# Entry of an experts' loop: the order of its first loads, splits and gate transfers

## The chip, the cores and the metric

One core of a Trainium2 chip runs the whole layer as one program. The metric is the device time of an execution in microseconds (us). "Before" and "change" are two programs that compute the same layer.

## What is computed

The reference is one layer of a streaming encoder: two token mixers (a gated DeltaNet and an HGRN2), merged by gates, then a product-key expert mixer, then a norm. The change lies where the mixer over experts begins. Cut to that part:

```
def _peer(x, w_pq, sub_keys, expert_u, expert_v):   # 512 tokens, D = 1024
    q = (xf @ w_pq).reshape(n_tok, P_HEADS, 2, P_DHALF)
    s = einsum('thpd,phkd->thpk', q, sub_keys)      # 8 heads, 2 x 128 keys
    ... top 16 of 256 candidate pairs of each head: idx, gate
    h = gelu(einsum('td,tkd->tk', xt, expert_u[idx]))
    y = einsum('tk,tkd->td', gate * h, expert_v[idx])
```

The kernel does this densely for the first 368 tokens: it computes h for all 16384 experts, multiplies by a gate that is zero nearly everywhere, and multiplies by all of expert_v. The other 144 tokens gather their own rows of expert_u and expert_v.

## The kernel before, in words

The 16384 experts are 128 blocks of 128. For a block b, TensorE makes h (128 experts by 368 tokens) from 8 x 3 matmuls, because each float32 operand is split in a high and a low part that TensorE takes as fp32r, and three of the four products are kept. ScalarE puts GELU(h) into one of 30 slots (tiles hext and ogA). Later block m multiplies its slot by the gates of its 128 experts (hg, line 1728), splits the product into wh and wl and the block of expert_v into vh and vl, and TensorE adds 18 matmuls into six accumulators y (y_part, y_mm). The products are taken in the order wh with vh, wh with vl, wl with vh, so the second matmul of a block needs vl, and the third wl.

Blocks 0 to 29 of h are made ahead of the loop, as filler for TensorE while the top-16 lists are formed and turned into dense gates. spread (line 1572 on) writes these gates, 12 slices of 32 tokens, to gD in DRAM: each slice goes through half of the tile stage, and of the last slice only the first 16 experts of each block row (256 KB) are written at once; the rest of it (1792 KB, called the gates' rest here) stays in stage for later.

The loop (line 1785) runs from i = -3 to 127, with n = i + 3. Each step loads block n of expert_v (v_load, line 1702) and the weights of h block n + 30 (w_load, line 482), issues gathers for the other tokens on GpSimd (line 1660), prepares block i + 1 (prep, line 1717) and gives TensorE the 18 y matmuls of block i and then the 24 matmuls of h block i + 30. Gates come back from gD four blocks at a time (g_load, line 1690): the first gate read, for blocks 0 to 3, on SyncE's queue, and the later ones on ScalarE's. Of these the second, for blocks 4 to 7, is issued at i = -1; its target lies in stage where the gates' rest still stands, and it reads rows of the rest too, so it waits for the write of the rest. This write (line 1807) follows at n = 1, and a one-element copy on GpSimd (line 1805, the probe), which reads the first gates and writes into stage, holds it until the first gate read has landed.

Splitting weights (w_split, line 485) is a copy on ScalarE for the high part (whi) and, for the low part (wlo), either a subtraction on VectorE or GpSimd, or, with eng None, a second ScalarE copy of -whi and an accumulating DMA from GpSimd's queue that adds the raw weights. The last 42 weights before the loop take the last way (w_cut).

prep for block 0 makes vh and wh on VectorE, for all others on ScalarE. Its order is hg, high parts, the split of h block m + 30, one gathered row if there is one (consume), wl, vl.

Every engine works its instructions in the order in which they are written in the source; in_order at the end of build fixes it. v 0, v 1, ... are blocks of expert_v, and h block 30 + m is made right behind the y part of block m.

Of the kernel before, what the change touches and what calls it, by code (L numbers as in the profile page):

```python
# [22 lines left out]
P = 128  # L23
# [20 lines left out]
NPRE = 30  # L44
# [29 lines left out]
NDMA = 4  # L74
# [5 lines left out]
GLEAD = 5  # L80
LAG = 2
GB = 4
# [197 lines left out]
def build(ctx, tc, I, O):  # L280
    nc = tc.nc
# [5 lines left out]
    def act(o, i, f, **kw):  # L287
        nc.scalar.activation(o, i, f, **kw)  # L288

    vec, gps, pe = nc.vector, nc.gpsimd, nc.tensor  # L290
# [172 lines left out]
    order = []  # L463
    for h in range(H):
        us = [(k, h) for k in HEAD]
# [6 lines left out]
    N0 = len(order)  # L472
# [5 lines left out]
    raws, wts = {}, {}  # L478

    def w_load(src):  # L480
        raw = wpool.tile([P, DC, UW], F32, tag="wraw", name="wraw")
        nc.sync.dma_start(raw, src)
        return raw

    def w_split(raw, eng=gps):
        hi = wpool.tile([P, DC, UW], F32R, tag="whi", name="whi")
        lo = wpool.tile([P, DC, UW], F32R, tag="wlo", name="wlo")
        act(hi, raw, AF.Copy)
        if eng is None:

            act(lo, hi.bitcast(F32), AF.Copy, scale=-1.0)
            gps.dma_start(out=lo, in_=raw, accum_op=OP.add)
        else:
            eng.tensor_tensor(lo, raw, hi.bitcast(F32), OP.subtract)  # L494
        return hi, lo
# [5 lines left out]

    def w_cut(n):
        if n < len(order):
            wts[n] = w_split(raws.pop(n), vec if n < 2 else gps if n < N0 + NDMA else None)

    def piece(p, w, c, m):
        whi, wlo = w
# [8 lines left out]
    with ExitStack() as ph:  # L516
        sb = ph.enter_context(tc.tile_pool(name="sb", bufs=1))

        def sbt(tag, bufs=1, shape=(P, T), dt=F32):
            return sb.tile(list(shape), dt, tag=tag, name=tag, bufs=bufs)  # L520
# [530 lines left out]
        for k in range((NF - 1) * DC):  # L1051
            n, c = 1 + k // DC, k % DC
            if n > NF - 3:

                c, n = divmod(k - (NF - 3) * DC, 2)
# [71 lines left out]
    with ExitStack() as ph:  # L1127
# [46 lines left out]
        for n in range(NPROJ, N0):  # L1174
# [10 lines left out]
            m = {"w_a": (ohi, olo), "w_b": hm, "w_out": (mhi, mlo)}.get(kind, hm)  # L1185
# [20 lines left out]
    gg2 = hk.tile([P, KP], F32, name="gg2")  # L1206
# [8 lines left out]
    def u_mm(uh, ul, p=None, part=(0, 3 * DC)):  # L1215
        p = psh.tile([P, ND], F32, tag="h", name="h") if p is None else p
        for i in range(*part):
            c, k = divmod(i, 3)
            mm(p[:, 0:NM], (uh, ul, uh)[k][:, c, :], (hhi, hhi, hlo)[k][:, c, 0:NM], i == 0, i == 3 * DC - 1)
        return p  # L1220

    def u_act(b, p):
        act(slots[b % NPRE][:, 0:NM], p[:, 0:NM], AF.Gelu)
# [10 lines left out]
    def cut(o, n, i=0):  # L1234
        return stage[:, o + i * n:o + (i + 1) * n]
# [13 lines left out]
    with ExitStack() as ph:  # L1249
# [68 lines left out]
        with ExitStack() as p2:  # L1318
# [117 lines left out]
            for n, (kind, j) in list(enumerate(order))[N0:]:  # L1436
# [12 lines left out]
                if adds:  # L1449
                    m = adds.pop(0)  # L1450
                    total(*m, vec)
                if muls:
                    m = muls.pop(0)
# [24 lines left out]
            while todo or muls or adds:  # L1478
                if adds:
                    total(*adds.pop(0), vec)  # L1480
                if muls:
                    m = muls.pop(0)
# [126 lines left out]
        for s in range(NS):  # L1609
# [6 lines left out]
            while done < want:  # L1616
                i = done % (3 * DC)
# [22 lines left out]
    with ExitStack() as ph:  # L1640
# [15 lines left out]
        def gather(k):  # L1656
            r = sbt("row", (D,), bufs=ROWB)
            kk = k % NK
            at = eidx[:, kk:kk + 1] if kk < H * KP else eidx2[:, kk - H * KP:kk - H * KP + 1]
            gps.indirect_dma_start(out=r, out_offset=None, in_=I["eu" if k < NK else "ev"],  # L1660
                                   in_offset=bass.IndirectOffsetOnAxis(ap=at, axis=0))
            return r
# [17 lines left out]
        NU = P - NPRE  # L1680

        def quota(i):
            if i <= 0:
                return 0
            n = min(i, NU)
            return min(2 * NK, int(n * R1) + int(math.ceil(max(i - NU, 0) * R2)))

        vraw, uraw, gbs, vs, ws, us, hp, rws = {}, {}, {}, {}, {}, {}, {}, {}

        def g_load(i, eng):  # L1690
            if i % GB == 0:
                gb = cut(3072, NA * GB * TS, i // GB % 2).rearrange("p (a n t) -> p a n t", n=GB, t=TS)
                eng.dma_start(gb.rearrange("p a n t -> p a (n t)"),
                              gD[0:NA, :, i:i + GB, :].rearrange("a p n t -> p a (n t)"))
                gbs[i // GB] = gb

        def v_load(i):
            if i < P - TAIL:
                vraw[i] = cut(0, D, i % 3)
            else:  # L1700
                vraw[i] = wpool.tile([P, DC, UW], F32, tag="wraw", name="wraw").rearrange("p a b -> p (a b)")
            nc.sync.dma_start(vraw[i], I["ev"][i * P:(i + 1) * P, :])
# [8 lines left out]
        def y_mm(i):  # L1711
            for tt in range(NT):
                for q in range(2):
                    y_part(i, tt, q)
            vs.pop(i), ws.pop(i)

        def prep(m, between=None):
            vr = vraw.pop(m)
            hg = sbt("hg", (ND,))
            if m < P - TAIL:  # L1720
                vh, vl = [sbt(k, (D,), F32R) for k in ("vh", "vl")]
                wh, wl = [sbt(k, (ND,), F32R) for k in ("wh", "wl")]
            else:

                vh, vl, w = [wpool.tile([P, DC, UW], F32R, tag=k, name=k).rearrange("p a b -> p (a b)")
                             for k in ("whi", "wlo", "whi" if m < P - 1 else "wlo")]
                wh, wl = w[:, 0:ND], w[:, ND:2 * ND]
            vec.tensor_tensor(hg.rearrange("p (a t) -> p a t", t=TS), slots[m % NPRE].rearrange("p (a t) -> p a t", t=TS),
                              gbs[m // GB][:, :, m % GB, :], OP.mult)
            if m == 0:  # L1730

                vec.tensor_copy(vh, vr)
                vec.tensor_copy(wh, hg)  # L1733
            else:
                act(vh, vr, AF.Copy)
                act(wh, hg, AF.Copy)
            if m < NU:
                us[m] = w_split(uraw.pop(m), vec)
            if between is not None:
                consume(between, rws.pop(between))  # L1740
            vec.tensor_tensor(wl, hg, wh.bitcast(F32), OP.subtract)
            vec.tensor_tensor(vl, vr, vh.bitcast(F32), OP.subtract)  # L1742
            vs[m], ws[m] = (vh, vl), (wh, wl)


# [2 lines left out]
        def x_load(tt):  # L1748
            xr[tt] = sbt("row", (D,), bufs=ROWB)
            nc.sync.dma_start(xr[tt], x2D[tt])  # L1750
# [34 lines left out]
        for i in range(-LEAD, P):  # L1785
            n = i + LEAD
            if i == P - TAIL - 1:
                assert not rws
                fn = sbt("row", (D,), bufs=ROWB)
                nc.sync.dma_start(fn, I["fnorm"].partition_broadcast(P))  # L1790
                for tt in (NT,) + tuple(range(NT)):
                    x_load(tt)
            if 0 < i + GLEAD < P:
                g_load(i + GLEAD, nc.scalar)
            if n < P - TAIL:
                v_load(n)
            if i == P - TAIL - EARLY - 1:
                for k in range(P - TAIL, P):
                    v_load(k)
            if n < NU:  # L1800
                uraw[n] = w_load(I["eut"][n + NPRE])
            if n == 0:
                g_load(0, nc.sync)

                gps.tensor_copy(cut(8512, 1), gbs[0][:, 0, 0, 0:1])
            if n == 1:
                nc.sync.dma_start(gD[NA - 1][:, 16:], gt[0][:, 16:])
            if i == 8:
                sx = junk[:, 0:P].bitcast(I32)
                vec.tensor_scalar(sx, ri, NX - 1, P - NX, OP.bitwise_and, OP.bitwise_or)  # L1810
                vec.tensor_tensor(selx, ci, sx, OP.is_equal)
            if 8 <= i < 8 + H:
                hr, hc = slice((i - 8) * NX, (i - 7) * NX), slice((i - 8) * KP, (i - 7) * KP)
                nc.sync.dma_start(eidx2[hr], ex[P - NX:P, hc])
                nc.sync.dma_start(gg2[hr], gs[P - NX:P, NT - 1, i - 8, :])
                nc.sync.dma_start(hx[hr], hxD)
            fresh = range(quota(i), quota(i + 1))
            for k in fresh:
                rws[k] = gather(k)
            todo = list(range(quota(i - LAG), quota(i - LAG + 1)) if i < P - TAIL - EARLY else sorted(rws))  # L1820
            if i - 1 in hp:
                u_act(i - 1 + NPRE, hp.pop(i - 1))
            if -1 <= i < P - TAIL - 1:
                prep(i + 1, *todo[:1])
                todo = todo[1:]
            if P - TAIL - EARLY <= i < P - EARLY:
                prep(i + EARLY)
            if 0 <= i < P - TAIL:
                y_mm(i)
                if i < NU:  # L1830
                    hp[i] = u_mm(*us.pop(i))
            for k in todo:
                consume(k, rws.pop(k))
            if i == P - TAIL:
                act(fn, fn, AF.Copy, scale=math.sqrt(D))
# [32 lines left out]
```

## Time and profile before

| what | value |
|---|---|
| median of 3 runs | 2093.02 us (2092.74 to 2094.04) |
| the profiled execution: its own time | 2093.28 us |
| its span, first to last instruction | 2091.1 us |
| TensorE busy | 2012.5 us, 96% of the span |
| VectorE, ScalarE, GpSimd busy | 1511.8, 940.7, 857.3 us |
| mean granted TensorE clock | 0.990 of full speed |

Times in the views are us from the span's start. In them PE is TensorE, PEld its loading of weights, DVE VectorE, ACT ScalarE, POOL GpSimd and SP SyncE; SPq, ACTq and POOLq are DMAs issued by these. "Idle before" is time in which an engine stood before the instruction, with what ended it. The work of all DMAs runs on 16 DMA engines; q1 is the queue of SyncE's DMAs, q10 that of ScalarE's, q0 that of GpSimd's. PEclk is the granted clock as a share of full speed (2.4 GHz; 0.5 is 1.2 GHz).

### The profile page before, as it was taken

To read this page: it belongs to the slowest core of one execution; us is meant where nothing else is said; L and a number is where in the kernel's file an instruction comes from. 1 tells how busy PE (TensorE), PEld (TensorE's weight loads), DVE (VectorE), ACT (ScalarE), POOL (GpSimd) and SP (SyncE) were. 2 spreads that over 40 slices of the span, in tenths; PEclk is the share of its full clock that TensorE was granted. 3 is DMA by queue.
4 is the path that set the end of the run, shared out by engine and by line. 5 is a ranking of instruction groups with operands and counts; after the bars stand their busy time and mean duration, and the time that the engine had idled before them with its cause. 6 is when DMAs were issued, how large, how long until landed. Compare 5 with 4: busy or idle time off the path is not lost.

```text
span 2091.1 us, 34918 instructions
## 1 busy us (share of the span) xinstructions
PE 2012.5 (96%) x13182; PEld 1729.2 (83%) x13182; DVE 1511.8 (72%) x2956; ACT 940.7 (45%) x1739; POOL 857.3 (41%) x863
## 2 busy tenths in 40 slices
PE   7899999999999999999798899999999999999998
PEld 5678787887878787888787799999999998898886
DVE  7666546656662366999996587787877878788887
ACT  4555555545554323566575333333333333333334
POOL 3566645655645644311101134334334433334522
PEclk9999999999999999999999999999999999999999
DMA  3322232132222543677799799999989989889996
GB/s 134 114 72 83 64 107 73 62 98 63 83 83 93 191 156 126 186 199 192 192 331 330 281 330 327 337 319 332 327 321 326 325 323 324 320 327 323 323 312 228
DMA packets 194873, 456.84 MB, mean 218 GB/s; under 512 B 28128, under 2 KB 91776, under 8 KB 193040
## 3 DMA queue, kind: packets, MB, share of 16 engines
q1 hardware_dynamic: 96016, 231.29, 31.0%
q0 software_dynamic: 47520, 173.04, 26.3%
q10 hardware_dynamic: 51168, 50.28, 7.3%
q8 instruction: 103, 1.69, 0.3%
q14 instruction: 66, 0.54, 0.1%
HBM read 393.11 MB, written 39.40 MB: 207 GB/s over the span
## 4 chain that ended last, share of the span: by engine, by line
PE 58%; DVE 14%; ACT 2%; issue 2%; DMA 2%; POOL 0%; SPq 0%; ACTq 0%; DVEq 0%; POOLq 0%
PE y L285 23%; PE h L285 19%; PE mm L285 12%; DVE Bg L1564 2%; DVE stage L1266 1%; DVE scr L1262 1%; DVE stage L1260 1%; DVE A L1560 1%; PE iv L285 1%; DMA gD<-stage 1%; DVE oh L1314 1%; PE pl L285 1%; DVE tv L1258 1%; DVE tv L1264 1%; PE mC L285 1%
## 5 line engine op out<-in xcount | busy, mean ns | idle before, releaser
L494 POOL TENSOR_TENSOR wlo<-wraw,whi 128x1024 fp32r<-128x1024 f32 x106 | 255.0, 2407 | 269.3 <-ACT whi L288 268.8
L285 PE MATMUL h<-hhi,wlo 128*128 128x368 f32 x1024 | 339.4, 331 | 6.2 <-DMA wlo<-wraw 6.2
L285 PE MATMUL h<-hhi,whi 128*128 128x368 f32 x1024 | 340.4, 332 | 2.0 <-ACT hext L288 1.9
L285 PE MATMUL h<-hlo,whi 128*128 128x368 f32 x1024 | 339.5, 332 | 1.6 <-POOL hlo L459 1.2
L285 PE MATMUL mm<-hhi,whi 128*128 128x512 f32 x792 | 328.8, 415 | 1.0 <-ACT a_k L288 0.6
L285 PE MATMUL mm<-hlo,whi 128*128 128x512 f32 x792 | 311.4, 393 | 4.2 <-POOL hlo L459 3.0
L288 ACT ACTIVATE whi<-wraw 128x1024 fp32r<-128x1024 f32 (+1 forms) x251 | 263.2, 1049 | 110.7 <-PE mm L285 46.1
L285 PE MATMUL mm<-hhi,wlo 128*128 128x512 f32 x792 | 309.6, 391 | 2.0 <-DMA wlo<-wraw 2.0
L285 PE MATMUL y<-vl,wh 128*128 128x512 f32 x756 | 297.7, 394 | 10.8 <-DVE vl L1742 10.5
L285 PE MATMUL y<-vh,wh 128*128 128x512 f32 x756 | 295.5, 391 | 4.8 <-DVE wh L1733 4.8
L285 PE MATMUL y<-vh,wl 128*128 128x512 f32 x756 | 296.5, 392 | 0.0
L1660 POOL DMA_INDIRECT row<-eu,eidx x144 | 172.6, 1199 | 285.5 <-DVE stage L1670 271.9
L1660 POOL DMA_INDIRECT row<-ev,eidx x144 | 174.9, 1215 | 275.0 <-DVE h2g L1678 219.0
L494 DVE TENSOR_TENSOR wlo<-wraw,whi 128x1024 fp32r<-128x1024 f32 x99 | 121.3, 1225 | 177.3 <-ACT whi L288 175.7
L285 PEld LDWEIGHTS h<-hhi,wlo 128*128 128x128 f32 x1024 | 193.7, 189 | 12.0 <-DMA wlo<-wraw 7.7
L285 PEld LDWEIGHTS h<-hhi,whi 128*128 128x128 f32 x1024 | 193.2, 189 | 6.9 <-ACT hext L288 2.5
L285 PEld LDWEIGHTS h<-hlo,whi 128*128 128x128 f32 x1024 | 193.3, 189 | 2.5 <-POOL hlo L459 1.8
L288 ACT ACTIVATE hext<-h 128x368 f32<-128x368 f32 x88 | 41.9, 476 | 334.6 <-PE h L285 329.3
L285 PEld LDWEIGHTS mm<-hlo,whi 128*128 128x128 f32 x792 | 148.7, 188 | 40.1 <-POOL hlo L459 4.7
L285 PEld LDWEIGHTS y<-vl,wh 128*128 128x128 f32 x756 | 142.3, 188 | 43.2 <-DVE vl L1742 16.2
L285 PEld LDWEIGHTS mm<-hhi,whi 128*128 128x128 f32 x792 | 149.0, 188 | 27.7 <-ACT a_k L288 1.0
L285 PEld LDWEIGHTS mm<-hhi,wlo 128*128 128x128 f32 x792 | 149.4, 189 | 26.5 <-DMA wlo<-wraw 2.3
(443 smaller groups left out, 3758.4 us busy)
## 6 DMA issues: line engine op xcount, KB each, us to landing
wraw<-eut SPq DMA_DIRECT2D x128, 512.0 KB
stage<-ev SPq DMA_DIRECT2D x126, 512.0 KB
wraw<-wu SPq DMA_DIRECT2D x119, 512.0 KB
stage<-gD ACTq DMA_DIRECT2D x31, 768.0 KB
gD<-stage ACTq DMA_DIRECT2D x11, 2048.0 KB
wlo<-wraw POOLq DMA_DIRECT2D x42, 512.0 KB
sg<-sgD SPq DMA_DIRECT2D x16, 256.0 KB
sgD<-tmpP SPq DMA_DIRECT2D x14, 256.0 KB
```

Source lines behind the costliest of these rows:

```text
L285: nc.tensor.matmul(o, l, r, start=start, stop=stop)
L288: nc.scalar.activation(o, i, f, **kw)
L494: eng.tensor_tensor(lo, raw, hi.bitcast(F32), OP.subtract)
L1258: vec.max(val[:, 0:8], src)
L1260: vec.max_index(idx[:, 0:8], val[:, 0:8], src)
L1262: vec.match_replace(scr, val[:, 0:8], src, -3.0e38)
L1264: vec.max(val[:, 8:16], scr)
L1266: vec.max_index(idx[:, 8:16], val[:, 8:16], scr)
L1314: eng.tensor_tensor(oh[:, :, 0:n, :], oh[:, :, 0:n, :], oh[:, :, n:2 * n, :], OP.add)
L1560: vec.tensor_tensor(A, it[:, 0, t0:t0 + TB].rearrange("p (n u) -> p n u", u=2)[:, :, None, :].to_broadcast([P, TP, P, 2]), iov[:, None, :, ...
L1564: vec.tensor_tensor(Bg[:, q].rearrange("p n a b u -> p (n a) b u"), hi[:, p1:p1 + TP].rearrange("p n a u -> p (n a) u")[:, :, None, :].to_ ...
L1660: gps.indirect_dma_start(out=r, out_offset=None, in_=I["eu" if k < NK else "ev"], in_offset=bass.IndirectOffsetOnAxis(ap=at, axis=0))
```

## The change

It edits five things at the entry. In prep for block 0 the split of h block 30 goes behind wl and vl of block 0. The first gate read moves ahead of the load of h block 30's weights. The gates' rest is written at n = 2 instead of 1, and the probe writes into gg2, which nothing reads before it is written again, so the write no longer waits for it. The second gate read is issued at i = 1 instead of -1. The last filler, h block 29, gets its low part by a subtraction on VectorE.

```
-            wts[n] = w_split(raws.pop(n), vec if n < 2 else gps if n < N0 + NDMA else None)
+            wts[n] = w_split(raws.pop(n), vec if n < 2 or n == len(order) - 1 else gps if n < N0 + NDMA else None)
...
-            if m < NU:
+            if 0 < m < NU:
                 us[m] = w_split(uraw.pop(m), vec)
             if between is not None:
                 consume(between, rws.pop(between))
             vec.tensor_tensor(wl, hg, wh.bitcast(F32), OP.subtract)
             vec.tensor_tensor(vl, vr, vh.bitcast(F32), OP.subtract)
+            if m == 0:
+                us[m] = w_split(uraw.pop(m), vec)
...
-            if 0 < i + GLEAD < P:
+            if i == 1:
+                g_load(GB, nc.scalar)
+            elif GB < i + GLEAD < P:
                 g_load(i + GLEAD, nc.scalar)
             if n < P - TAIL:
                 v_load(n)
...
+            if n == 0:
+                g_load(0, nc.sync)
+                gps.tensor_copy(gg2[:, 0:1], gbs[0][:, 0, 0, 0:1])
             if n < NU:
                 uraw[n] = w_load(I["eut"][n + NPRE])
-            if n == 0:
-                g_load(0, nc.sync)
-                gps.tensor_copy(cut(8512, 1), gbs[0][:, 0, 0, 0:1])
-            if n == 1:
+            if n == 2:
                 nc.sync.dma_start(gD[NA - 1][:, 16:], gt[0][:, 16:])
```

On VectorE, behind the last lists of expert numbers, the rows were these (wraw_12686 holds h block 30's weights, hg_12698 and vh_12699 belong to block 0, hg_12719 to block 1):

```order
L1632 CAST ex_8712<-posf_12583 128x128
L1728 TENSOR_TENSOR hg_12698<-hext_8716,stage_8721 128x384
L1732 CAST vh_12699<-stage_8721 128x1024
L1733 CAST wh_12701<-hg_12698 128x384
L494 TENSOR_TENSOR wlo_12707<-wraw_12686,whi_12706 128x1024
L1741 TENSOR_TENSOR wl_12702<-hg_12698,wh_12701 128x384
L1742 TENSOR_TENSOR vl_12700<-stage_8721,vh_12699 128x1024
L1728 TENSOR_TENSOR hg_12719<-hext_8716,stage_8721 128x384
```

and are now these (wraw_12430 holds h block 29's weights, wraw_12687 block 30's):

```order
L1632 CAST ex_8712<-posf_12583 128x128
L494 TENSOR_TENSOR wlo_12587<-wraw_12430,whi_12586 128x1024
L1728 TENSOR_TENSOR hg_12696<-hext_8716,stage_8721 128x384
L1732 CAST vh_12697<-stage_8721 128x1024
L1733 CAST wh_12699<-hg_12696 128x384
L1741 TENSOR_TENSOR wl_12700<-hg_12696,wh_12699 128x384
L1742 TENSOR_TENSOR vl_12698<-stage_8721,vh_12697 128x1024
L494 TENSOR_TENSOR wlo_12707<-wraw_12687,whi_12706 128x1024
L1728 TENSOR_TENSOR hg_12717<-hext_8716,stage_8721 128x384
```

The low part of h block 30 has gone behind wl and vl of block 0, and that of h block 29 has come in ahead of hg.

On SyncE, at the loop's first steps, the DMAs were issued in this order (ev is expert_v, eut the weights of h blocks, 12686, 12691 and 12696 those of blocks 30 to 32):

```order
L1702 DMA stage_8721<-ev 128x1024
L482 DMA wraw_12686<-eut 128x1024
L1693 DMA stage_8721<-gD_105 128x12x128
L1702 DMA stage_8721<-ev 128x1024
L482 DMA wraw_12691<-eut 128x1024
L1807 DMA gD_105<-stage_8721 128x3584
L1702 DMA stage_8721<-ev 128x1024
L482 DMA wraw_12696<-eut 128x1024
```

and now:

```order
L1702 DMA stage_8721<-ev 128x1024
L1693 DMA stage_8721<-gD_105 128x12x128
L482 DMA wraw_12687<-eut 128x1024
L1702 DMA stage_8721<-ev 128x1024
L482 DMA wraw_12690<-eut 128x1024
L1702 DMA stage_8721<-ev 128x1024
L482 DMA wraw_12693<-eut 128x1024
L1813 DMA gD_105<-stage_8721 128x3584
```

The first gate read is second instead of third, and the write of the gates' rest stands behind v 2 and h block 32's weights.

On ScalarE, from the GELUs of the last fillers on (whi_12706 is the high part of h block 30, whi_12727 and whi_12725 that of block 31), one piece of the difference:

```order
-L288 ACTIVATE wlo<-whi 128x1024
 L288 ACTIVATE ogA<-h 128x368 x4
-L1693 DMA stage<-gD 128x12x128
-L288 ACTIVATE whi<-wraw 128x1024
-L288 ACTIVATE vh<-stage 128x1024
-L288 ACTIVATE wh<-hg 128x384
-L288 ACTIVATE whi<-wraw 128x1024
+L288 ACTIVATE whi<-wraw 128x1024
+L288 ACTIVATE vh<-stage 128x1024
+L288 ACTIVATE wh<-hg 128x384
+L288 ACTIVATE whi<-wraw 128x1024
+L1693 DMA stage<-gD 128x12x128
 L288 ACTIVATE hext<-h 128x368
```

The second gate read has gone from ahead of h block 30's high part to behind h block 31's; the GELU of h block 30 is next behind it.

## Rows read from the trace of the kernel before

**Rows 1.** Busy time by stage, of the entry and of the loop.
```profile
1142.30:1147.00 4.70, 0.00 (x0) 0.01 (x1) 1.43 (x3) 0.47 (x1) 1.23 (x2) 0.96 0.80 308
1147.50:1157.30 9.80, 0.28 (x1) 0.00 (x0) 2.88 (x4) 2.00 (x2) 3.87 (x5) 0.50 0.99 365
1157.30:1162.70 5.40, 5.40 (x17) 4.36 (x18) 3.71 (x5) 1.47 (x2) 0.00 (x0) 0.72 1.04 400
...
1400.00:2000.00 600.00, 598.71 (x3053) 537.10 (x3053) 482.65 (x575) 211.79 (x295) 243.48 (x198) 1.00 0.91 324
```

**Rows 2.** Timeline of TensorE: start us, us, engine, line, operation [idle before, releaser].
```profile
1138.15 0.43 PE L285 MATMUL h<-hhi,wlo 128*128 128x368 f32 x1 [0.42 <-DMA wlo<-wraw]
...
1147.02 0.76 PE L285 MATMUL y<-vh,wh 128*128 128x512 f32 x1 [4.77 <-DVE wh L1733]
1157.30 0.79 PE L285 MATMUL y<-vl,wh 128*128 128x512 f32 x1 [9.52 <-DVE vl L1742]
...
1174.82 0.39 PE L285 MATMUL y<-vh,wh 128*128 128x512 f32 x1
...
1191.05 0.39 PE L285 MATMUL y<-vh,wh 128*128 128x512 f32 x1
```

**Rows 3.** The chain that ended last, at the entry: start us, us, what.
```profile
1136.64 8.68 DMA stage<-gD
...
1146.07 6.81 DMA gD<-stage
```

**Rows 4.** Timeline of VectorE at the entry.
```profile
1145.44 0.56 DVE L1728 TENSOR_TENSOR hg<-hext,stage 128x384 f32<-128x384 f32 x1 [16.84 <-DMA stage<-gD]
...
1146.52 0.35 DVE L1733 CAST wh<-hg 128x384 fp32r<-128x384 f32 x1
...
1170.86 0.55 DVE L1741 TENSOR_TENSOR wl<-hg,wh 128x384 fp32r<-128x384 f32 x1
1171.33 1.22 DVE L1742 TENSOR_TENSOR vl<-stage,vh 128x1024 fp32r<-128x1024 f32 x1
...
1182.87 0.55 DVE L1728 TENSOR_TENSOR hg<-hext,stage 128x384 f32<-128x384 f32 x1
...
1188.70 1.22 DVE L1742 TENSOR_TENSOR vl<-stage,vh 128x1024 fp32r<-128x1024 f32 x1
```

**Rows 5.** Timeline of ScalarE at the entry.
```profile
1152.90 0.38 ACTq L1693 DMA_DIRECT2D stage<-gD  x1
...
1166.90 0.48 ACT L288 ACTIVATE hext<-h 128x368 f32<-128x368 f32 x1 [7.69 <-PE h L285]
```

**Rows 6.** Timelines of SyncE (two rows) and GpSimd (one).
```profile
1135.07 0.33 SPq L1702 DMA_DIRECT2D stage<-ev  x1
...
1172.62 0.33 SPq L1702 DMA_DIRECT2D stage<-ev  x1
...
1146.35 1.22 POOL L1660 DMA_INDIRECT row<-eu,eidx  x1 [0.31 <-DVE hg L1728]
```

**Rows 7.** DMA view of 1134.5:1137, 1137:1140, 1140:1143, 1146.5:1151.5, 1153:1155, 1168:1169, 1173:1174.
```profile
q0 software_dynamic: 124, 0.51, 111.6%
...
q1 hardware_dynamic: 273, 1.01, 88.8%
...
DMA packets 1441, 0.84 MB, mean 281 GB/s; under 512 B 23, under 2 KB 1408, under 8 KB 1441
...
DMA packets 134, 1.86 MB, mean 371 GB/s; under 512 B 1, under 2 KB 1, under 8 KB 6
q1 hardware_dynamic: 134, 1.86, 107.5%
...
q0 software_dynamic: 101, 0.41, 52.7%
q1 hardware_dynamic: 112, 0.39, 49.3%
...
q10 hardware_dynamic: 24, 0.01, 3.5%
...
DMA  0000000000000000000000090996400909904907
```

Columns of rows 1: stretch and its length, then busy us and instructions of PE, PEld, DVE, ACT and POOL, PEclk, busy share of the DMA engines, GB/s. Columns of a queue's row in rows 7: packets, MB, share of the 16 engines' time; the last row is the busy share of the DMA engines in 40 slices of its stretch, in tenths.

## The prediction

> **What bounds the kernel now.** I read the table by stage first. Over most of the experts' loop TensorE is busy 598.7 of 600 us [rows 1], so there nothing is to be had; at the loop's entry it is idle from 1142.25 to 1157.3 but for one matmul, and its clock is then granted at 0.50 of full speed, mean 0.72 over the 5.4 us after it [rows 1]. TensorE's own rows split the idle time: 4.77 us until wh of block 0, 9.52 us until vl of block 0 (the second matmul), and earlier 0.42 us until the low part of h block 29's weights [rows 2]. The chain of waits says where those come from. The first gate read, issued at 1136.64, takes 8.68 us and lands at 1145.32; the write of the last gates' rest starts only then, at 1146.07, and takes 6.81 us [rows 3]. ScalarE stands before the second gate read until that write lands, and issues it at 1152.90 [rows 5]; only behind it come h block 30's high part, VectorE's wlo, wl and vl, and the second matmul. wl and vl of block 0 need nothing of this: vh and wh were ready at 1146.87 [rows 4].
>
> **Term 1, wlo of h block 30 behind block 0's low parts.** From the landing of the first gate read, T, VectorE now goes hg, vh, wh, wl, vl without a wait. By [rows 4] hg starts 0.12 us after T, hg to the end of wh takes 1.43 us, wl starts 0.47 us ahead of vl, and vl takes 1.22 us: T + 3.25; with 0.05 us to TensorE the second matmul starts at T + 3.3. All behind it slides with it: from the second matmul to the first of block 2 pass 1174.82 − 1157.30 = 17.5 us without an idle row [rows 2]. I keep that stretch with its slow clock, since some 3 us of idle time remain ahead of it.
>
> **Term 2, when T falls.** v 0's load is issued at 1135.07 as before [rows 6]; then comes the gate read, ahead of h block 30's weights. In the trace of before, queue q0 (GpSimd's accumulating transfer for h block 29) has the engines alone from 1134.5 to 1137; v 0 and h block 30's weights then move 1.01 MB in 3 us, and 1408 small packets, nearly all the gate read's, move in the next 3 us [rows 7]. So from 1137.1 to the landing pass 8.2 us, of which block 30's weights are 1.45; without them 6.75. Where does v 0 start now that the accumulating transfer is gone? The load issued at 1172.62 [rows 6], on idle engines, shows its first busy slice as the 24th of 40 in the us from 1173 [rows 7], 1.0 us after its issue: 1136.1. The bounds are 1135.1, no delay at all, and 1137.1, the old start. I take 1136.1, the nearest row, so T = 1142.9 (1141.9 to 1143.85), and the second matmul at 1146.2 in place of 1157.30: **11.1 us** earlier.
>
> **Term 3, the second gate read.** It now stands on ScalarE behind the high parts of h blocks 30 and 31, and it still waits for the write of the gates' rest; call its landing X. SyncE issues that write behind two more loads and without the wait for the first gates. Queue order from v 0 at 1136.1: v 0 1.45 us, gate read 3.1, five loads at 1.4, together until 1147.7; the write itself moves 1.86 MB in 5.0 us [rows 7] and lands 1.4 us after its last packet (1152.88 against 1151.5): X = 1154.1 if nothing cuts in. The gathers, first issued 1.0 us after T [rows 3, 6], can: from 1153 to 1155, q0 and q1 take turns, 101 packets to 112 [rows 7]. v 2, h block 32's weights and the write have eight packets an engine each, so at most three gathers of 1.3 us fit between: X = 1158.0. But from 1146.5 to 1151.5, with gathers issued from 1146.35 on, all 134 packets were q1's [rows 7]: the write went through whole. I take the middle, 1156.1. Queued behind the read on ScalarE are h block 30's GELU, vh and wh of block 2 and h block 32's high part; from that GELU to the end of block 2's vl it is 1172.55 − 1166.90 = 5.65 us [rows 4, 5], so block 2 can start at X + 6.1 = 1162.2. By term 2 TensorE gets there at 1146.2 + 17.5 = 1163.7. The read is in time by 1.5 us, and costs nothing up to X = 1157.6.
>
> **Edits at nothing.** wlo of h block 29 on VectorE (1.2 us, as vl of the same shape) falls into the 16.84 us in which VectorE waits for the first gates [rows 4]; ScalarE loses a copy. The 0.42 us before h block 29's low part goes, but TensorE then waits for T anyway; it would count only if T came before 1140. Block 30's weights come 3.1 us later in the queue; they are needed at 1151.6, when the y part of block 0 ends, and VectorE makes their wlo right behind vl at 1147.4: 4 us in hand. v 3 moves behind the write, at about X + 3 = 1159; its copy on ScalarE is due at 1164. The probe on GpSimd only writes elsewhere.
>
> **Where the next wait can be.** The second gate read is first used by hg of block 4. From that hg to the end of vl pass 7.1 us (1182.87 to 1189.92), and block 4 starts at 1191.05 [rows 2, 4]: it must land by 1191.05 − 11.1 − 7.1 = 1172.8. In the trace of before it was issued at 1152.90 and its queue q10 still had 24 packets from 1168 to 1169 [rows 5, 7], 16 us. From 1156.5 that makes 1172.5. No margin; the traffic around it is as large as then but starts earlier, so I put no cost, and each us more is a us lost.
>
> **Sum.** 11.1 us off the profiled execution's 2093.28 us (span 2091.1 and 2.2 around it) makes 2082.2; the median of the runs is 0.26 us below that execution, so **2081.9 us**.
>
> **The rivals.**
> The first read comes no earlier. Its 1536 small packets are the slow part, and some engines finish later than others: 1408 small ones had moved by 1143, and yet it landed 2.3 us later. With T left at 1145.32 term 1 alone stays: second matmul at 1148.6, 8.7 us gained, 2084.3. Against it: 512 KB less stands ahead of it, and q0's transfer is gone. Chance 0.12.
>
> The gathers push the write back, and ScalarE stands at the second read. If all five of them (6.5 us) go ahead of the write's end, X = 1160.6, or 1161.6 with v 0 starting at 1137.1; block 2 starts at 1166.7 to 1167.7, 7 to 8 us gained, 2085.5. For it: the gathers now come while three q1 transfers still wait; against it: the 5 us of [rows 7] in which the gathers moved nothing. Chance 0.13. The Trainium skill (DMA: Bandwidth & Descriptors, "Queues, rings and completion order") says that a DMA engine goes round its queues packet by packet, which speaks against this change; by that alone X would be 1158.0 and the gain 10.7 us. The trace agrees from 1153 on (101 to 112), and not from 1146.5 to 1151.5.
>
> Slower: the second read itself starves. It has 96 small packets an engine (1536 over 16). If each waits for one 4 KB packet of q0 and one of q1 (0.16 us each at the 0.81 MB in 2 us of [rows 7], and 0.03 its own), it takes 34 us, lands at 1191 and puts block 4 at 1198, 7 us later than before: 2100. It decides from a landing at 1184 on, 27 us after issue. Against it: 16 us in the trace of before, beside five gathers and four loads. Chance 0.04. A landing between 1174 and 1180 costs a part of the gain: chance 0.05, 2084 to 2089.
>
> Two of these at once leave less than 4.2 us, 0.2% of the time and about what a measurement of this kernel can tell from no change: chance 0.04.
>
> **How the numbers follow.** The forecast has 0.62. With the three rivals that keep a gain (0.12, 0.13, 0.05) faster has 0.92, same 0.04, slower 0.04. Lower end: T at 1141.9, and the 17 matmuls at full clock (0.23 us apart, 4.1 instead of 5.4 us): 13.4 us gained, 2079.6, if X is below 1155.3 (block 2 at 1161.4). Upper end: the gathers' case with 1 us more, 2086.5; past it lie the last two cases and parts of two others, some 0.15.
>
> **What would show it.** Right: TensorE's second y matmul at about 1146 with no idle row over 2 us ahead of it but one for wh; the first gate read issued by 1136 and landing by 1143.9; no wait named wlo<-wraw on TensorE at h block 29; block 2's first matmul near 1163.7; the second read issued on ScalarE near 1156 and hg of block 4 without a wait for it. Wrong: a wait of ScalarE for the gates' write that TensorE's row for block 2 shows as idle time; VectorE waiting for stage<-gD a second time; or a first read that still lands at 1145.

## The result and the profile after

| | before | change |
|---|---|---|
| median | 2093.28 us (2092.33 to 2094.37, 6 runs) | 2081.32 us (2078.54 to 2082.02, 6 runs) |
| profiled execution: its own time | 2093.28 us | 2081.32 us |
| its span | 2091.1 us | 2079.4 us |
| TensorE busy | 2012.5 us | 2012.6 us |

The ratio is 0.994, with a 95% interval from 0.9927 to 0.9953: faster by 12.0 us, 0.6%. The forecast was 2081.9 us. Two slow executions, one of before (5647.55 us) and one of the changed kernel run again (2643.80 us), are left out of the medians below. TensorE is busy for as long as before, so all of the gain is idle time.

Busy time by stage of the change (columns as in [rows 1]): the idle time at the entry, the block behind it, the block after that, and the loop.

```profile
1140.50:1144.40 3.90, 0.50 (x3) 0.21 (x2) 3.20 (x6) 2.28 (x3) 2.65 (x3) 0.91 1.02 417
1144.40:1150.40 6.00, 6.00 (x14) 4.74 (x15) 4.46 (x6) 1.78 (x3) 4.20 (x4) 0.50 1.06 445
1150.40:1155.20 4.80, 4.80 (x28) 4.57 (x28) 0.36 (x1) 0.00 (x0) 0.00 (x0) 0.98 0.97 399
1400.00:2000.00 600.00, 598.67 (x3044) 536.39 (x3043) 482.31 (x574) 211.66 (x295) 240.22 (x197) 1.00 0.90 324
```

The loop is what it was (598.7 of 600 us). TensorE now stands still for 3.4 us of 3.9, where [rows 1] had it so from 1142.25 to 1157.3; but then it runs for 6 us at a granted clock of 0.50, its lower level, and comes back to full speed only after that.

TensorE's timeline of the change, three rows: the first two y matmuls of block 0 and the first of block 2, the answers to [rows 2].

```profile
1142.75 0.47 PE L285 MATMUL y<-vh,wh 128*128 128x512 f32 x1 [2.23 <-DVE wh L1733]
1144.38 0.79 PE L285 MATMUL y<-vl,wh 128*128 128x512 f32 x1 [1.17 <-DVE vl L1742]
1163.34 0.39 PE L285 MATMUL y<-vh,wh 128*128 128x512 f32 x1
```

The 4.77 and 9.52 us have become 2.23 and 1.17; the wait for h block 29's low part is gone. Block 2 begins 11.48 us earlier (1174.82 to 1163.34), and the span is 11.7 us shorter: what is won at the entry is kept to the end. Of the 11.48 us, 1.10 lie ahead of every edited instruction in this pair of executions: the last gate slice's write is issued at 1130.25 before and at 1129.15 now (its rows are shown with the experiments).

The chain that ended last, of the change, at the entry ([rows 3]):

```profile
1129.15 5.01 DMA gD<-stage
...
1134.36 6.69 DMA stage<-gD
...
1143.11 1.23 DVE vl L1742
1144.34 0.04 issue
1144.38 7.02 PE y L285 x17
1151.40 4.00 PE h L285 x24
```

The chain goes from the write of the last gate slice to the first gate read, through VectorE's five operations, and on along TensorE. The write of the gates' rest, 6.81 us of the chain in [rows 3], is not in it any more.

VectorE of the change ([rows 4]):

```profile
1130.62 1.23 DVE L494 TENSOR_TENSOR wlo<-wraw,whi 128x1024 fp32r<-128x1024 f32 x1 [2.70 <-ACT whi L288]
1141.17 0.56 DVE L1728 TENSOR_TENSOR hg<-hext,stage 128x384 f32<-128x384 f32 x1 [9.32 <-DMA stage<-gD]
...
1143.11 1.22 DVE L1742 TENSOR_TENSOR vl<-stage,vh 128x1024 fp32r<-128x1024 f32 x1
1144.24 1.22 DVE L494 TENSOR_TENSOR wlo<-wraw,whi 128x1024 fp32r<-128x1024 f32 x1
...
1171.40 0.55 DVE L1728 TENSOR_TENSOR hg<-hext,stage 128x384 f32<-128x384 f32 x1
```

From hg to vl nothing waits, wlo of h block 29 lies in the wait for the first gates, wlo of h block 30 follows vl at once, and hg of block 4 (1171.40) does not wait for the second gate read.

ScalarE of the change ([rows 5]): the second gate read and h block 30's GELU behind it.

```profile
1153.19 0.38 ACTq L1693 DMA_DIRECT2D stage<-gD  x1
1155.44 0.48 ACT L288 ACTIVATE hext<-h 128x368 f32<-128x368 f32 x1 [8.01 <-PE h L285]
```

The GELU behind the read waits for TensorE's h, not for the read: the read is in time by 2.2 us.

### The profile page after: what moved, and what is told of

Same layout as the page of the kernel before. It is cut to its first block, busy times and chain, and to the rows that moved or that the text cites. A ratio compares the mean times of both kernels' runs of the same rounds, so it can differ in the third digit from the quotient of the medians.

```text
span 2079.4 us, 34912 instructions
## 1 busy us (share of the span) xinstructions
PE 2012.6 (97%) x13182; PEld 1728.6 (83%) x13182; DVE 1512.4 (73%) x2957; ACT 940.6 (45%) x1738; POOL 856.8 (41%) x862
## 4 chain that ended last, share of the span: by engine, by line
PE 51%; DVE 18%; issue 4%; ACT 3%; DMA 1%; POOL 0%; DVEq 0%; ACTq 0%; POOLq 0%; SPq 0%
PE y L285 20%; PE h L285 15%; PE mm L285 13%; DVE h2g L1678 3%; DVE Bg L1564 2%; DVE vl L1742 1%; ACT whi L288 1%; DVE stage L1266 1%; DVE A L1560 1%; DVE scr L1262 1%; DVE stage L1260 1%; PE iv L285 1%; DVE oh L1314 1%; PE pl L285 1%; DVE tv L1258 1%
```

## The experiments

The theory: four pieces make the gain. The split behind the low parts takes the second gate read out of block 0's path; the read's later place takes it out of h block 30's path; the earlier place of the first gate read and the dropped accumulating transfer bring the first gates earlier. The main rival: one of these does it all. A second question came out of the traces: what the slow clock behind the remaining idle time costs, and what becomes the bound once it is gone.

A single trace is not enough for a question of 1 us, since everything up to the entry lies earlier or later by some 3 us between executions: the issue of the last gate slice's write, on ScalarE's queue (line 1588), lies between 1129.15 and 1132.45 in the twelve traces, though nothing ahead of it was edited. So I measure from this event of the same execution. Its rows of before and of the change:

```profile
1130.25 0.33 ACTq L1588 DMA_DIRECT2D gD<-stage  x1
```

```profile
1129.15 0.33 ACTq L1588 DMA_DIRECT2D gD<-stage  x1
```

The start of hg of block 0 less this issue is called the gate delay: 1145.44 − 1130.25 = 15.19 us before, 1141.17 − 1129.15 = 12.02 now. All medians below are of executions on the same chip as the runs of before that give the ratio; e8 and e9 ran on another chip than the other eight.

| run | edit | gate delay, us | median, us | ratio to before, 95% |
|---|---|---|---|---|
| e1_split_only | before, with the split alone | 14.22 | 2087.34 | 0.9958 to 0.9983 |
| e2_second_read_early | change, second read early | 12.44 | 2090.09 | 0.9968 to 0.9987 |
| e3_read_third | change, first read third | 13.03 | 2083.05 | 0.9938 to 0.9966 |
| e4_filler_dma | change, accumulating transfer | 12.45 | 2081.64 | 0.9932 to 0.9960 |
| after_again | change, unedited | 11.47 | 2081.84 | 0.9923 to 0.9948 |
| e5_y_by_product | change, block 0's products in turn | 11.32 | 2078.70 | 0.9914 to 0.9939 |
| e6_read_first | change, first read ahead of v 0 | 10.33 | 2081.76 | 0.9928 to 0.9954 |
| e7_both | e5 and e6 | 10.91 | 2081.28 | 0.9924 to 0.9949 |
| e8_product_write_at_1 | e5, rest written a step earlier | 11.51 | 2077.50 | 0.9917 to 0.9944 |
| e9_both_write_at_1 | e7, rest written a step earlier | 10.49 | 2078.70 | 0.9918 to 0.9945 |

### The split alone

```
-            if m < NU:
+            if 0 < m < NU:
                 us[m] = w_split(uraw.pop(m), vec)
...
+            if m == 0:
+                us[m] = w_split(uraw.pop(m), vec)
```

> The kernel before with one edit: the split of h block 30 goes behind wl and vl of block 0. Theory (two waits in a row): the second matmul comes 3.3 us after the first gate read lands, at about 1148.6, but ScalarE still stands before the second gate read until about 1153, so the low part of h block 30 is ready at 1155.6 and y of block 1 starts at about 1160.6 instead of 1166.70: some 6 us less than before, about 2087. Rival (the wait for vl was all of it): the whole 8.7 us, about 2084.5, with y of block 1 at 1158.

Measured: 2087.34 us, 6.63 below the 2093.97 of before beside it. TensorE's and ScalarE's rows:

```profile
1149.10 0.80 PE L285 MATMUL y<-vl,wh 128*128 128x512 f32 x1 [1.16 <-DVE vl L1742]
1154.89 0.43 PE L285 MATMUL h<-hhi,whi 128*128 128x368 f32 x1 [0.30 <-ACT whi L288]
1156.15 0.44 PE L285 MATMUL h<-hhi,wlo 128*128 128x368 f32 x1 [0.83 <-DVE wlo L494]
1160.99 0.50 PE L285 MATMUL y<-vl,wh 128*128 128x512 f32 x1 [0.49 <-DVE vl L1742]
```

```profile
1153.78 1.06 ACT L288 ACTIVATE whi<-wraw 128x1024 fp32r<-128x1024 f32 x1 [8.64 <-DMA gD<-stage]
```

The theory holds. The second matmul starts 8.2 us earlier than in [rows 2], but ScalarE still stands 8.64 us before the second gate read, and h block 30's high part, its low part and block 1's vl now each hold TensorE for 0.3 to 0.8 us. The split alone gives a little over half of the gain.

### The second read early again

```
-            if i == 1:
-                g_load(GB, nc.scalar)
-            elif GB < i + GLEAD < P:
+            if GB < i + GLEAD < P:
                 g_load(i + GLEAD, nc.scalar)
...
                 nc.sync.dma_start(gD[NA - 1][:, 16:], gt[0][:, 16:])
+                g_load(GB, nc.scalar)
```

> The changed kernel, with the second gate read on ScalarE ahead of h block 30's high part again, behind the write of the gates' rest in the program. Theory: ScalarE stands until that write lands near 1153, h block 30's low part comes at 1155.6, y of block 1 at 1160.8 instead of 1155.25: 5.6 us more than the changed kernel, about 2087. Rival (the second read is off the path wherever it stands): as the changed kernel, 2081.3.

Measured: 2090.09 us (2086.68 to 2092.25, 11 runs), some 8 us above the change. Rows of TensorE and ScalarE, then of the chain, then the stretch of h block 30 by stage, in the profiled execution (the longest of the 11):

```profile
1158.29 0.44 PE L285 MATMUL h<-hhi,whi 128*128 128x368 f32 x1 [4.42 <-ACT whi L288]
```

```profile
1157.18 1.06 ACT L288 ACTIVATE whi<-wraw 128x1024 fp32r<-128x1024 f32 x1 [12.91 <-DMA gD<-stage]
```

```profile
1142.38 14.32 DMA gD<-stage
...
1159.55 6.79 PE h L285 x23
```

```profile
1160.00:1162.00 2.00, 2.00 (x8) 2.00 (x8) 0.50 (x1) 1.47 (x2) 0.00 (x0) 0.50 1.03 384
```

The direction is the theory's, the size is larger. The wait is of the expected kind, 4.42 us before h block 30's high part; but TensorE's clock is granted at 0.50 after it, and h block 30's 23 remaining matmuls take 6.79 us, where such a block takes 4.00 for 24 at full clock, or 3.83 for 23. Those 3.0 us were missing from my sum. So the later place of the second read is worth more than the two steps that bring the first gates earlier: without it they gain nothing over the split alone (2087.34), since the write that ScalarE stands for ends no earlier: at 1156.70 in this trace, 24.3 us after the issue of the last gate slice's write, where before had 1152.88, 22.6 us after it.

### The first read third, and the accumulating transfer back

```
-            if n == 0:
-                g_load(0, nc.sync)
-                gps.tensor_copy(gg2[:, 0:1], gbs[0][:, 0, 0, 0:1])
             if n < NU:
                 uraw[n] = w_load(I["eut"][n + NPRE])
+            if n == 0:
+                g_load(0, nc.sync)
+                gps.tensor_copy(gg2[:, 0:1], gbs[0][:, 0, 0, 0:1])
```

> The changed kernel, with the first gate read behind h block 30's weights again. Theory (queue order on q1 sets when the read lands): it lands one load of 512 KB later, 1.45 us, and all behind it too: about 2082.8. Rival (the read waits for the write of the last gate slice, its place behind it is worth nothing): 2081.3, with the read landing as early as in the changed kernel.

```
-vec if n < 2 or n == len(order) - 1 else
+vec if n < 2 else
```

> The changed kernel, with the low part of h block 29 by ScalarE and the accumulating transfer again. Theory (512 KB on q0 ahead of v 0): the first gate read lands about 1 us later, at most 2.5 us, and the 0.42 us wait at h block 29 comes back but is hidden: about 2082.3. Rival (nothing of the gain comes from this edit): 2081.3.

> The changed kernel unedited, as the measure for the three beside it on the same chip: 2081.3, between 2080 and 2083.

Measured: 2083.05 and 2081.64 us, beside 2081.84 for the change, run again later on that chip. The intervals overlap, so the times don't tell these apart. The gate delay does better. The programs with the first read second (change, its repeat, e2, e5, e8) have 12.02, 11.47, 12.44, 11.32 and 11.51: mean 11.75. With the read third it is 13.03, 1.3 more than the mean and beyond all five; with the accumulating transfer back it is 12.45, 0.7 more, which the highest of the five has too. TensorE's row shows the transfer's direct cost, which the subtraction on VectorE had removed:

```profile
1138.83 0.43 PE L285 MATMUL h<-hhi,wlo 128*128 128x368 f32 x1 [0.76 <-DMA wlo<-wraw]
```

In this trace the wait is covered: the last filler ends at 1142.9, just as the first gates land. So each of the two steps rests on one trace, and only the read's place lies outside the spread of the others.

### Block 0's products in turn

Now the 1.17 us between the first and the second matmul. The accumulators allow all six vh-wh products of block 0 first, then six with wl, then six with vl; vl is then needed some 3 us later.

```
+            if i == 0:
+                (vh, vl), (wh, wl) = vs[0], ws[0]
+                for k, (w, v) in enumerate(((wh, vh), (wl, vh), (wh, vl))):
+                    for tt in range(NT):
+                        for q in range(2):
+                            mm(py[2 * tt + q], w[:, tt * P:(tt + 1) * P], v[:, q * T:(q + 1) * T], k == 0, False)
+            else:
                 ...
```

> The changed kernel, with block 0's 18 y matmuls ordered by product: the six of wh with vh first, then wl with vh, then wh with vl. Theory (1.17 us of idle time before vl remain, and the slow clock costs more behind it): the six fill that gap, 1.2 us less; if TensorE's shorter idle time also keeps the clock at full speed, up to 4 us less, 2077 to 2080. Rival (the entry is held by the second gate read now): no difference.

Measured: 2078.70 us (2077.86 to 2079.45), 3.1 below the 2081.84 of the unedited change beside it. Four of the change's five executions there lie from 2080.98 to 2082.43 us; the fifth, at 2078.52, lies among e5's, as one of the change's first six does (2078.54), and no trace of such an execution shows why. TensorE, VectorE, and the stretch by stage:

```profile
1142.80 1.62 PE L285 MATMUL y<-vh,wh 128*128 128x512 f32 x6 [1.59 <-DVE wh L1740]
1144.26 1.54 PE L285 MATMUL y<-vh,wl 128*128 128x512 f32 x6
...
1159.86 0.50 PE L285 MATMUL y<-vl,wh 128*128 128x512 f32 x1 [0.34 <-DVE vl L1749]
```

```profile
1169.65 0.56 DVE L1735 TENSOR_TENSOR hg<-hext,stage 128x384 f32<-128x384 f32 x1 [2.40 <-DMA stage<-gD]
```

```profile
1142.00:1144.00 2.00, 1.20 (x5) 1.05 (x6) 1.97 (x4) 1.38 (x2) 1.58 (x2) 1.00 1.03 420
1144.00:1146.00 2.00, 2.00 (x10) 1.63 (x9) 1.99 (x3) 0.74 (x1) 1.70 (x2) 1.00 1.04 385
```

The second idle row is gone, and the clock stays at 1.00. The chain of after_again has the stretch with which it compares:

```profile
1146.12 5.76 PE y L285 x17
```

In this repeat of the change the 17 matmuls behind the idle time took 5.76 us and in the change's first profile 7.02, against some 4.1 at full clock: 1.7 and 2.9 us more. Beside the repeat, 1.17 us of idle time and 1.7 us of slow clock make 2.9 of the 3.1 us. Whether the clock stays up because TensorE stands still for less (1.59 us instead of 2.85) or because no lone matmul lies between two waits, this run doesn't tell. New limits show: vl of block 2 makes TensorE wait (0.34 us) since the second gate read is issued on ScalarE only at 1153.73, and VectorE waits 2.40 us for its landing.

### The first read ahead of v 0

```
+            if n == 0:
+                g_load(0, nc.sync)
+                gps.tensor_copy(gg2[:, 0:1], gbs[0][:, 0, 0, 0:1])
             if n < P - TAIL:
                 v_load(n)
```

with VectorE's order for block 0 now hg, wh, wl, vh, vl, since v 0 comes last.

> The changed kernel, with the first gate read issued ahead of v 0, and block 0's order on VectorE hg, wh, wl, vh, vl. Theory (the read's place on q1 sets its landing): it lands 1.3 us earlier, v 0 lands behind it, and the second matmul comes 1.3 us earlier: about 2080.0. Rival (the read is held by the write of the last gate slice and by its own small packets): 0.5 us or nothing.

> The two edits together. Theory: 2.5 us less than the changed kernel, about 2078.8, and if the clock stays at full speed some 3 us more, until the second gate read holds block 2 at its landing + 6.1 us. Rival: no more than the better of the two alone.

Measured: 2081.76 us alone, 2081.28 together with the products in turn, so neither is told apart from the change. The gates did come earlier (gate delays 10.33 and 10.91). Alone, in the fastest of its five executions (2079.77 us, the profiled one), TensorE still has two idle rows, and the clock falls behind them, to 0.51 from 1146 to 1148:

```profile
1142.89 0.47 PE L285 MATMUL y<-vh,wh 128*128 128x512 f32 x1 [1.26 <-DVE vh L1734]
1144.06 0.50 PE L285 MATMUL y<-vl,wh 128*128 128x512 f32 x1 [0.70 <-DVE vl L1744]
```

Together, the time that is won ahead is lost at block 2. The chain and TensorE of e7_both:

```profile
1139.52 16.17 DMA gD<-stage
...
1161.89 5.77 PE y L285 x17
```

```profile
1143.31 1.62 PE L285 MATMUL y<-vh,wh 128*128 128x512 f32 x6 [1.89 <-DVE vh L1741]
...
1161.89 0.50 PE L285 MATMUL y<-vl,wh 128*128 128x512 f32 x1 [1.89 <-DVE vl L1751]
```

The first gates release GpSimd's gathers too. In this trace the write of the gates' rest is issued 0.8 us later than in e5 (1139.52 against 1138.72) and takes 16.17 us against 14.93. The gathers move 0.99 MB beside it from 1145 to 1154.3, against 0.52 MB in e5 from 1145 to 1152.3, which fits the longer time; no run shows it apart from the rest. The second gate read is issued at 1155.77, 2 us later than in e5; block 2 waits 1.89 us, and its 17 matmuls take 5.77 us at a reduced clock.

### The rest written one step earlier

```
-            if n == 2:
+            if n == 1:
                 nc.sync.dma_start(gD[NA - 1][:, 16:], gt[0][:, 16:])
```

> Block 0's matmuls by product as in e5_y_by_product, and the gates' rest written one step earlier, ahead of v 2 and h block 32's weights (1 MB, some 2.9 us of transfers). Theory (in e5 the second gate read had become the bound of block 2, by 0.3 us of wait and perhaps more in other executions): the read is issued at about 1151 instead of 1153.7, no row of block 2 waits, and the time falls by 0.4 to 1 us, to about 2078. Rival (v 2 and h block 32's weights are late now: vh of block 2 and the high part of h block 32 want them on ScalarE from about 1152 on): a wait for stage<-ev or wraw<-eut takes the place of the other, no gain or up to 2 us more.

> As e7_both, with the gates' rest written one step earlier. Theory (in e7 the earlier gathers pushed the write back, the read went out at 1155.77, block 2's second matmul waited 1.89 us for vl and its 17 matmuls then took 5.8 instead of some 4.1 us): read issued at about 1153, block 2's second matmul without a wait, clock kept: 2.5 to 3.5 us less than e7's 2081.3, about 2078. Rival (the loads behind the write are late, as in e8; or the gathers push the write back by as much as it was moved forward): 2080 to 2082.

Measured: 2077.50 us (2076.75 to 2080.51) and 2078.70 us (2077.63 to 2079.03). The chains of e8 and e9:

```profile
1136.74 12.54 DMA gD<-stage
1149.32 19.52 DMA stage<-gD
1168.86 0.57 DVE hg L1735
```

```profile
1138.29 12.69 DMA gD<-stage
1151.00 19.84 DMA stage<-gD
```

ScalarE of e9, vh of block 2 and the high part of h block 32:

```profile
1153.60 1.06 ACT L288 ACTIVATE vh<-stage 128x1024 fp32r<-128x1024 f32 x1 [1.55 <-DMA stage<-ev]
...
1156.22 1.06 ACT L288 ACTIVATE whi<-wraw 128x1024 fp32r<-128x1024 f32 x1 [1.15 <-DMA wraw<-eut]
```

The theory holds for the read's issue: 1149.3 and 1151.0 instead of 1153.7 and 1155.8. The rival's waits come too, on ScalarE: 0.65 and 1.22 us in e8, where TensorE does not feel them, and 1.55 and 1.15 us in e9, where they, and no longer the read, leave TensorE a wait of 0.31 us at block 2. e9 keeps its clock. Its median is 2.6 us below e7's, but on another chip; measured against before, the two are not told apart (ratios 0.9931 and 0.9937, each with about 0.0013 to either side). But now the second gate read itself is in the chain: issued earlier, it takes 19.5 to 19.8 us beside the gathers and loads, and hg of block 4 waits for it until 1168.86. e8 has the lowest median of all, 4.3 us below the change run again, but on another chip; the runs don't tell e5, e8 and e9 apart (ratios 0.9926, 0.9931 and 0.9931, each with about 0.0013 to either side). All three beat before; e5 is the one that was timed beside the change on one chip, and its median there is 3.1 us lower.

## Why the prediction was right

**The bound, and term 1: right.** TensorE's second y matmul started at the first gates' landing plus 3.33 us (1144.38 − 1141.05; 3.33 in the repeat too), predicted 3.3. e1 shows that the split is a gain by itself, 6.6 us.

**Its stretch of 17.5 us: right to 1.5 us.** "I keep that stretch with its slow clock" was the choice. From the second matmul to block 2 it took 18.96 us in the change's profile and 17.71 in its repeat. The slow clock did stay, although the idle time fell from 14.3 to 3.4 us, and it cost up to 1.4 us more than behind the long break. The lower end of the range (17 matmuls at full clock) was not seen in the change's two traces, but e5 shows that it can be had.

**Term 2: its direction right, its size too small.** I had the first gates land at 1142.9, which is a gate delay of 12.8; it is 11.75 in the mean. Of the two parts, the place ahead of h block 30's weights came out as 1.3 us (1.45 predicted), and the accumulating transfer as 0.7 (1.0 predicted), which one trace does not tell from the spread. Their sum, 2.0, is less than the 3.4 from before's 15.19; e1, whose order up to the first gates is before's, has 14.22, so a good part of the difference lies in the spread of single traces. The two profiles split their own 3.2 us in this way: the read is issued 5.21 us behind the slice's write instead of 6.39 (1134.36 − 1129.15 and 1136.64 − 1130.25; h block 30's load ahead of it had held SyncE for 0.96 us), and it is in flight 6.69 us instead of 8.68. The prediction also has no term for a wait that the chain of the change shows: the read goes out only when the last gate slice's write has landed, at 1134.16, 0.5 us after v 0's load.

So the sum was met partly by luck: the gates came about 1 us sooner than predicted, and the stretch behind them was 0.2 to 1.5 us longer. Counted from the slice's write, the first matmul of block 2 comes 10.4 us earlier in the change's profile (34.19 us instead of 44.57) and 12.2 in its repeat (32.39), where the prediction had 11.1; the profile's 11.48 has the 1.10 us from ahead of the entry in it.

**Term 3: right that the read costs nothing, wrong about why.** I took X = 1156.1, it was 1153.19; from the landing of the first gates that is 12.1 us against the 13.2 of the prediction. By the prediction's own count (X + 6.1 against the first matmul of block 2) 4.0 us were in hand in the profile and 2.5 in the repeat (X = 1155.26, block 2 at 1163.83), not 1.5. What failed is the reading of [rows 7] that "the write went through whole". The DMA view of the change, 1147 to 1150, while the write moves:

```profile
q1 hardware_dynamic: 67, 0.95, 73.6%
q0 software_dynamic: 67, 0.27, 22.2%
```

One packet of the gathers goes for each packet of the write. In the trace of before no gather's packet appears until the us from 1152, 5.7 us after the first gather's issue at 1146.35; in the change they appear from the us from 1146 on, 4 us after the issue at 1142.06. The DMA row of before from 1151 to 1152 tells why its write met none:

```profile
DMA  0099999090990990000000000000000000000000
```

The write's last packets end at about 1151.4, the engines then stand empty to the end of that us, and still no gather's packet moves. The write met no gathers because they were not there yet, not because it had precedence. The Trainium skill (DMA: Bandwidth & Descriptors, "Queues, rings and completion order") has it that an engine goes round its queues packet by packet, and the trace agrees, 67 to 67. By that rule alone I would have set X = 1158.0, 15.1 us behind the first gates' landing; it came 12.1 us behind it, because little of the gathers' traffic fell into the write: 0.50 MB from 1145.5 to 1151.5, at the 432 GB/s of that stretch 1.2 us.

**The second read's landing: in time.** I had feared 16 us in flight and no margin. It was 12.9 in the profile and 15.5 in the repeat, and hg of block 4 did not wait in either. The rows of the DMA view from 1153.2 to 1165 show its company:

```profile
q1 hardware_dynamic: 559, 2.03, 43.0%
q0 software_dynamic: 499, 1.78, 37.0%
q10 hardware_dynamic: 1545, 0.78, 24.9%
```

Its 0.78 MB go through in 12 us beside 3.8 MB of the two others. The slower rival (34 us in flight) was wrong, but its place was right: in e5, e8 and e9 this read, with 15.9 to 19.8 us, is what is late next, though only VectorE feels it so far: TensorE has one wait at block 4, of 0.27 us, in e9.

**"Block 2 can start at X + 6.1": confirmed**, for its second matmul, where the read was late: in e5 1159.86 − 1153.73 = 6.13, in e7 1161.89 − 1155.77 = 6.12.

**Edits at nothing: right.** wlo of h block 29 lay in VectorE's wait, h block 30's weights did not hold TensorE, and v 3 did not either.

## What to carry to other kernels

An issue that waits for a write is a wait for everything written behind it on the same engine: put it behind the work that needs nothing of it, as far back as its own landing allows, and work that landing out before moving it. When an idle gap gets short, count what the clock gives up behind it: here the last 1.2 us of waiting cost 1.7 to 2.9 us more, and an order of products that let TensorE run on was worth more than another transfer brought forward. A transfer that comes earlier also releases whoever waits for it: follow those transfers to the next deadline before counting the gain.

## What was not expected of the hardware

The granted clock behind short breaks. In the change TensorE stood 2.23 and 1.17 us with one matmul between, and the clock was then at 0.50 for some 7 us; in its repeat (1.68 and 1.17 us) and in e6 (1.26 and 0.70 us) it was there for some 3 us. In e5, e8 and e9 TensorE stood once, 1.59, 1.72 and 1.44 us, and then had matmuls without a break, and the clock stayed at 1.00. So it did in e7 behind its first stop, of 1.89 us; but behind its second, also 1.89 us, the clock fell to 0.50 for some 3 us, though 17 matmuls followed without a break. The length of a stop alone does not settle it, and these traces don't show what does. In e2 stops of 4.42 and 0.82 us, with one matmul between, made the next 23 matmuls take 6.79 us.

The write of 1792 KB took 6.81 us alone ([rows 3]) and 12.5 to 16.2 us from issue to landing where loads stood ahead of it and gathers beside it. The second gate read, 768 KB in small packets, took 12.9 us in the change and 19.8 in e9: in e8 it was issued 4.4 us earlier than in e5, and hg of block 4 started only 0.8 us earlier (1168.86 against 1169.65).
